# Dense attention with a subtracted maximum: reductions over 1024 keys, the maxima carried by DMA as one row, and the sums of the exponentials added up by a pair of half-width products

## The chip, the cores and the metric

The kernel runs on one core of a Trainium2 chip. The metric is the device time of one execution in microseconds (us), the median of several runs. Matrix products run on TensorE (PE in the profile; PEld is its weight loading), the other arithmetic on VectorE (DVE), ScalarE (ACT) and GpSimd (POOL). All transfers of the part discussed here are issued on one queue, that of SyncE (SP), in program order.

## The reference, cut to what matters

Two layers of a diffusion backbone, 2048 tokens behind a prefix of 256 context tokens, width 1024. The change lies in the dense attention of the first layer: 8 query heads of 64 channels share 2 key/value heads, and every query sees 2304 keys (256 context keys, then 2048 others). Context queries see the 256 context keys alone.

```python
def dense_attn(q, k, v):
    ...
    qg = q.reshape(Bq, Lq, Hk, Hq // Hk, dh)
    s = jnp.einsum('bqkgd,bskd->bkgqs', qg, k).astype(jnp.float32) * (dh ** -0.5)
    p = jax.nn.softmax(s, axis=-1).astype(v.dtype)
    o = jnp.einsum('bkgqs,bskd->bqkgd', p, v)
    return o.reshape(Bq, Lq, Hq * dh)
```

The softmax is computed with the row's maximum subtracted before the exponential and the row's sum divided out after the product with the values. The program keeps scores with the opposite sign, so that the maximum is a minimum (`ALU.min`), and `AF.Exp` runs with scale -1.

## The kernel before, in words

The program runs its phases one after another: `ab_proj` (input projection, convolution), `ab_attention`, `ab_out`, then the second layer. Only `load_kv` and `ab_attention` are touched.

**Units.** The work is cut into 36 units in the list `units` (L850 to L852), one for 256 queries of two query heads: 512 columns of queries. 32 units see 18 tiles of 128 keys; four (block 0, the context queries) see 2 tiles. They run one after another, 584 tiles in all.

**What one tile of keys costs.** `score` (L902) multiplies one tile of keys by the unit's 512 queries into one PSUM bank of the pool `ps_s` (two banks, used in turn). It is two products: one over 128 rows with the rounded queries and keys, and one over the tile `qm` and the low part of the keys, whose last rows add the (negated) maximum: the keys' tile has rows of ones there (L803), `qm` has the shift. `exp` on ACT (L912) reads the bank and writes `pr`. `multiply` (L915) takes two tiles of `pr` at a time: the values of either tile have 64 columns, so that the two products fill the two halves of the array's columns and land in partitions 0 to 63 and 64 to 127 of one bank (`ps_a`). `add` (L932) adds up the `pr` tiles, some on DVE (`accd`), the rest on POOL (`accp`).

**The maxima ahead of it.** `chunk` (L876) computes the rounded scores the other way round, 128 queries in the partitions and up to 512 keys in the columns, into one of three banks (`ps_m`), and DVE reduces each to one column (L886). A unit has 4 tiles of queries by 5 chunks (four of 512 keys, one of 256). `least` (L888) takes the least of five columns. `shift_row` (L892) transposes the [128, 4] result on PE into a bank of the pool `ps_r`, and one DVE instruction spreads it, times an identity, over the rows 64 to 67 of `qm`.

**The sums behind it.** `join` (L949) adds `accd` and `accp` on POOL. `sum_high` and `sum_low` split the sum into two rounded parts on ACT and DVE. `total` (L966) multiplies both by a column of ones into the bank of `ps_r` (one row of 512 sums), ACT copies the row, and a transfer (L980) spreads it over 128 partitions. `invert` (L982) takes the reciprocal, writes it to DRAM (L987) and reads it back broadcast over 128 partitions (L989). `divide`, `fold` and `store` (L991 to L1007) finish the unit on POOL and ACT. In the last unit `total` uses 128 columns of ones and inverts the full tile on DVE.

**What sets the order.** The instructions of TensorE, ScalarE, VectorE and GpSimd are issued in an order written out by hand: every tile of keys is one step, `at(step, order, f)` files each piece of work under a step and a rank within it (L1009 to L1036), and L1079 to L1085 emit them step by step, ranks in ascending order (maxima and their rows 0, 1, 4, 5; score and exponential 2; multiply 3; add 6; the unit's tail 7). The tail's distances from the unit's last step `e` stand in `CHAIN`; `RATE` is the number of steps from one chunk to the next, and a unit's last chunk is `AHEAD` = 7 steps before its first score. The order on SP is chosen by a scheduler. `extra` (L1058) fits other work into the same steps: conditioning products (`adaln`), writes of a bias table to DRAM (`patterns`, L268), the output projection's weights, and parts of the convolution's normalization.

PSUM has eight banks: three for chunks, two for scores, one for the product with the values, one for rows (`ps_r`), one for the other work (`ps_c`).

Of the kernel before, what the change touches and what calls it, by code (L numbers as in the profile page):

```python
# [83 lines left out]
class Build:  # L84
# [705 lines left out]
    def load_kv(self):  # L790

        nc = self.nc
        self.kv_es = ExitStack()
        kp = self.pool(self.kv_es, "kp", 1, side="right")
        self.kt = []
        for kv in range(2):
            rows = slice(kv * 64, kv * 64 + 64)
            hi = kp.tile([P, T], F32R, name=f"k{kv}h")
            lo = kp.tile([68, T], F32R, name=f"k{kv}l")
            for r in range(2):  # L800
                nc.sync.dma_start(hi[r * 64 : r * 64 + 64].bitcast(F32), self.k_d[0, rows])
            nc.sync.dma_start(lo[0:64].bitcast(F32), self.k_d[1, rows])
            nc.vector.tensor_copy(  # L803
                lo[64:68].rearrange("p (a n) -> p a n", n=P),
                self.ones[64:68].unsqueeze(1).broadcast_to((4, NT, P)),
            )
            self.kt.append((hi, lo))
        self.vt = kp.tile([P, NT, P], F32, name="vt")
        nc.sync.dma_start(self.vt[:], self.v_d[:].rearrange("i p n -> p i n"))

    def ab_attention(self):
# [7 lines left out]
        with ExitStack() as es:  # L819
# [9 lines left out]
            tp = self.pool(es, "apt", 6)  # L829
# [13 lines left out]
            onesr = rp.tile([P, P], F32R, name="onesr")  # L843
            nc.vector.tensor_copy(onesr[:], self.ones[:])
            AHEAD, LAG, SUM, RATE, ROW = 7, 3, 2, 0.85, 4
# [3 lines left out]
            CHAIN = (5, 7, 9, 11, 14, 19, 21, 22)  # L849
# [12 lines left out]
            def load_q(i):  # L862
                b, hp = units[i]
                qs = qp.tile([P, 2, 256], F32R, name="q", tag="q")
                for j in range(2):
                    nc.sync.dma_start(qs[:, j].bitcast(F32), self.qs_d[2 * hp + j][:, b * 256 : b * 256 + 256])
                st = sp.tile([P, 4, 6], F32, name="ast", tag="ast")
                state[i] = {"q": qs, "st": st}

            def load_high(i):  # L870
                b, hp = units[i]
                qm = state[i]["qm"] = mp.tile([68, 2, 256], F32R, name="qm", tag="qm")
                for j in range(2):
                    nc.sync.dma_start(qm[0:64, j].bitcast(F32), self.qs_d[2 * hp + j][0:64, b * 256 : b * 256 + 256])

            def chunk(i, qt, c):  # L876

                b, hp = units[i]
                s = state[i]
                a = c * 512  # L880
                n = min(512, tiles[i] * P - a)
                lhs = s["q"][:, qt // 2, (qt % 2) * P : (qt % 2) * P + P]
                ps = ps_m.tile([P, 512], F32, name="m", tag="m")
                nc.tensor.matmul(ps[:, :n], lhs, kt[hp // 2][0][:, a : a + n], start=True, stop=True)  # L884
                col = c if b else 5
                nc.vector.tensor_reduce(out=s["st"][:, qt, col : col + 1], in_=ps[:, :n], axis=AX.X, op=ALU.min)  # L886

            def least(i):  # L888
                st = state[i]["st"]
                nc.vector.tensor_reduce(out=st[:, :, 5:6], in_=st[:, :, 0:5], axis=AX.X, op=ALU.min)  # L890

            def shift_row(i):  # L892
                s = state[i]
                pt = ps_r.tile([P, 512], F32, name="row", tag="row")
                nc.tensor.transpose(pt[0:4, 0:P], s["st"][:, :, 5], self.ident[:])
                nc.vector.scalar_tensor_tensor(
                    out=s["qm"][64:68].rearrange("p j (i n) -> p (j i) n", n=P),
                    in0=pt[0:4, 0:P].unsqueeze(1).broadcast_to((4, 4, P)), scalar=-1.0,
                    in1=self.ident[0:4, 0:4].unsqueeze(2).broadcast_to((4, 4, P)), op0=ALU.mult, op1=ALU.mult,
                )  # L900
# [14 lines left out]
            def multiply(i, k):  # L915
                b, hp = units[i]
                s = state[i]
                if k == 1:
                    s["av"] = ps_a.tile([P, 512], F32, name="av", tag="av")
                kv = hp // 2  # L920
                for x in range(2):
                    nc.tensor.matmul(  # L922
                        s["av"][x * 64 : x * 64 + 64], vt[:, k - 1 + x, kv * 64 : kv * 64 + 64], s["pr"][k - 1 + x][:],
                        start=k == 1, stop=k == tiles[i] - 1,
                    )
# [5 lines left out]

            def add(i, k):  # L932

                s = state[i]
                n = tiles[i]
                if n == 2:
                    mine, eng, name = [0, 1], nc.vector, "accd"
                else:
                    dve = [3 * x + 2 for x in range(5)] + [16, 17] if i < len(units) - 1 else list(range(TAIL, n))
                    mine, eng, name = (dve, nc.vector, "accd") if k in dve else ([x for x in range(n) if x not in dve], nc.gpsimd, "accp")  # L940
# [8 lines left out]
            def join(i):  # L949
                s = state[i]  # L950
                if "accp" in s:
                    nc.gpsimd.tensor_tensor(out=s["accd"][:], in0=s["accd"][:], in1=s["accp"][:], op=ALU.add)

            def sum_high(i):
                s = state[i]
                s["sh"] = rp.tile([P, 512], F32R, name="sh", tag="sh")
                nc.scalar.activation(s["sh"][:], s["accd"][:], AF.Copy)

            def sum_low(i):
                s = state[i]  # L960
                s["sl"] = rp.tile([P, 512], F32R, name="sl", tag="sl")
                nc.vector.tensor_tensor(
                    out=s["sl"][:], in0=s["accd"][:], in1=s["sh"][:].bitcast(F32), op=ALU.subtract
                )

            def total(i):  # L966

                s = state[i]
                pt = ps_r.tile([P, 512], F32, name="row", tag="row")
                m = 1 if i < len(units) - 1 else P  # L970
                for x in ("sh", "sl"):
                    nc.tensor.matmul(pt[0:m], onesr[:, 0:m], s[x][:], start=x == "sh", stop=x == "sl")
                if m == P:
# [3 lines left out]
                row = rp.tile([1, 512], F32, name="srow", tag="srow")  # L977
                nc.scalar.activation(row[:], pt[0:1], AF.Copy)
                s["rc"] = sp.tile([P, 4], F32, name="rc", tag="rc")
                nc.sync.dma_start(s["rc"][:], row[0:1].rearrange("o (p f) -> o p f", f=4))  # L980

            def invert(i):  # L982
# [3 lines left out]
                nc.vector.reciprocal(s["rc"][:], s["rc"][:])  # L986
                nc.sync.dma_start(self.inv_d[i % 2].rearrange("o (p f) -> (o p) f", f=4), s["rc"][:])  # L987
# [23 lines left out]
            for i in reversed(range(len(units))):  # L1011
                chunks = [(qt, c) for qt in range(4) for c in range(5 if units[i][0] else 1)]
                time = min(time - RATE, first[i] - AHEAD)
                last = int(time // 1)
                for x in reversed(chunks):
                    at(int(time // 1), 4, bind(chunk, i, *x))
                    begin = int(time // 1)
                    time -= RATE
                time += RATE
                at(begin - 3, 0, bind(load_q, i))  # L1020
                at(last - 2, 0, bind(load_high, i))
                if units[i][0]:
                    at(last + 1, 5, bind(least, i))
                at(last + ROW, 1, bind(shift_row, i))
            for i, n in enumerate(tiles):
                for k in range(n):
                    s = first[i] + k
                    at(s, 2, bind(score, i, k))
                    if k % 2 == 1:
                        at(s + LAG + 0, 3, bind(multiply, i, k))  # L1030
# [865 lines left out]
```

## Time and profile before

| | us |
|---|---|
| three runs | 2920.73, 2907.32, 2914.79; median 2914.79 |
| the profiled execution | 2907.36, of it the span of the profile 2905.6 |
| first score product of the attention | at 703.4 of the span |
| last score product of the attention | at 1532.7 |
| mean granted TensorE clock over the span | 0.977 |

In the profile's groups a line gives the source line, engine, operation, the tiles written and read, their shapes, a count, then the busy time in us and the mean duration of one instruction in ns, then the engine's idle time ahead of that group and what ended it. A product counts as busy until its modelled end, although the next one can start earlier: the distance between two starts is what a product costs on PE when PE is the limit. In a timeline the columns are the start in us, the duration in us, engine, line and operation; "x4" merges four of a kind. The table by stretches gives the busy time of each engine in each stretch, then the granted clock, the busy share of the DMA engines and GB/s.

### The profile page before, as it was taken

Reading aid. Unit: us, or ns where it says so; the run is one execution under the profiler, and the core shown is the slowest. Engines: PE = TensorE matmul, PEld = TensorE weight load, DVE = VectorE, ACT = ScalarE, POOL = GpSimd, SP = SyncE. Lnnn points to the kernel's source line nnn. Section 1 sums busy time; section 2 is a strip of 40 time slices with the busy share of each in tenths; the row PEclk is TensorE's granted clock in tenths of the full one; section 3 lists DMA queues with packets and bytes.
Section 4 is the critical chain, followed back from the end, with each engine's and each line's share of the span. In section 5 each row is a group of like instructions: output and inputs, shape, how many; then the busy total and the mean of one; then the engine's idle time right before and its main releaser. Section 6 shows DMA issues by size and latency. Waiting matters only on the chain.

```text
span 2905.6 us, 40946 instructions
## 1 busy us (share of the span) xinstructions
PE 2752.1 (95%) x14481; PEld 2118.0 (73%) x14481; DVE 1825.2 (63%) x2867; ACT 1116.8 (38%) x2081; POOL 1416.4 (49%) x1151
## 2 busy tenths in 40 slices
PE   7998799999999999999999999999999997889898
PEld 5988799996444444444447788988898876788787
DVE  4798868898777878878977454101212246777563
ACT  3223120312445555555553223123222236677321
POOL 2568610711666787887885652222222214445342
PEclk9999899998999999999999999999999998999999
DMA  9546332474533433321216543333434269998862
GB/s 297 192 131 207 129 123 97 135 239 151 149 107 103 144 98 106 120 68 44 73 33 210 192 159 143 138 112 112 143 132 136 82 197 230 235 230 196 270 210 80
DMA packets 346808, 432.27 MB, mean 149 GB/s; under 512 B 55900, under 2 KB 260236, under 8 KB 341611
## 3 DMA queue, kind: packets, MB, share of 16 engines
q1 hardware_dynamic: 310891, 403.03, 46.2%
q10 hardware_dynamic: 35712, 26.62, 2.9%
q8 instruction: 114, 1.87, 0.3%
q14 instruction: 91, 0.75, 0.1%
HBM read 281.87 MB, written 152.84 MB: 150 GB/s over the span
## 4 chain that ended last, share of the span: by engine, by line
PE 62%; DMA 10%; DVE 3%; POOL 2%; issue 2%; ACT 1%; SPq 0%; POOLq 0%; ACTq 0%; DVEq 0%
PE av L922 9%; PE s L907 8%; PE mm L431 6%; PE mm L433 6%; PE mm L432 6%; PE m L884 6%; PE mo L1107 4%; PE mo L1108 4%; PE mo L1109 4%; DMA nv<-v_d 3%; DMA nk<-k 3%; PE mm L442 1%; PE mm L441 1%; PE mm L440 1%; DMA pat<-pat_d 1%
## 5 line engine op out<-in xcount | busy, mean ns | idle before, releaser
L886 DVE TENSOR_REDUCE ast<-m 128x1 f32<-128x512 f32 (+1 forms) x656 | 397.9, 626 | 145.9 <-PE m L884 143.8
L912 ACT ACTIVATE pr<-s 128x512 f32<-128x512 f32 x584 | 343.2, 595 | 311.7 <-PE s L907 269.6
L947 POOL TENSOR_TENSOR accp<-accp,pr 128x512 f32<-128x512 f32 x283 | 400.1, 1414 | 86.0 <-ACT pr L912 71.3
L447 POOL TENSOR_TENSOR wlo<-wraw,whi 128x1024 fp32r<-128x1024 f32 x64 | 202.4, 3169 | 380.3 <-ACT whi L446 380.2
L533 DVE SCALAR_TENSOR_TENSOR acc<-u,cw,acc 128x1151 f32<-128x1151 f32 (+1 forms) x240 | 353.0, 1526 | 0.0
L922 PE MATMUL av<-pr,vt 128*64 128x512 f32 x1168 | 315.7, 619 | 0.0
L433 PE MATMUL mm<-hi_ab,wlo 128*128 128x384 f32 x768 | 258.7, 338 | 16.8 <-POOL wlo L447 15.5
L432 PE MATMUL mm<-lo_ab,whi 128*128 128x384 f32 x768 | 259.8, 339 | 0.0
L431 PE MATMUL mm<-hi_ab,whi 128*128 128x384 f32 x768 | 256.2, 340 | 3.3 <-ACT hi_ab L380 1.9
L431 PE MATMUL mm<-hi_cd,whi 128*128 128x512 f32 x640 | 250.8, 392 | 1.1 <-ACT hi_cd L380 1.1
L432 PE MATMUL mm<-lo_cd,whi 128*128 128x512 f32 x640 | 250.1, 391 | 0.4 <-DVE lo_cd L381 0.4
L433 PE MATMUL mm<-hi_cd,wlo 128*128 128x512 f32 x640 | 246.7, 390 | 0.0
L947 DVE TENSOR_TENSOR accd<-accd,pr 128x512 f32<-128x512 f32 x165 | 169.2, 1026 | 1.3 <-DVE accd L947 0.5
L1664 DVE TENSOR_TENSOR nlo<-npt,nhi 128x512 fp32r<-128x512 f32 x192 | 123.6, 645 | 69.3 <-ACT nhi L1662 68.5
L884 PEld LDWEIGHTS m<-k1h,q 128*128 128x128 f32 x328 | 61.8, 188 | 133.8 <-DVE ast L886 79.8
L433 PEld LDWEIGHTS mm<-hi_ab,wlo 128*128 128x128 f32 x768 | 145.5, 190 | 17.8 <-POOL wlo L447 15.8
L884 PEld LDWEIGHTS m<-k0h,q 128*128 128x128 f32 x328 | 63.5, 196 | 125.2 <-DVE ast L886 82.1
L1626 POOL TENSOR_SCALAR npr<-npr,nst 128x640 f32<-128x640 f32 (+1 forms) x128 | 108.0, 857 | 89.5 <-DVE nst L1625 64.1
L372 DVE TENSOR_SCALAR ht<-ptr,scale,shift 128x384 f32<-128x384 f32 (+2 forms) x96 | 61.2, 671 | 141.1 <-PE ptr L369 140.5
L431 PEld LDWEIGHTS mm<-hi_ab,whi 128*128 128x128 f32 x768 | 144.9, 190 | 5.3 <-ACT hi_ab L380 2.9
L432 PEld LDWEIGHTS mm<-lo_ab,whi 128*128 128x128 f32 x768 | 145.4, 189 | 0.9 <-issue 0.8
L431 PEld LDWEIGHTS mm<-hi_cd,whi 128*128 128x128 f32 x640 | 120.4, 188 | 26.1 <-ACT hi_cd L380 1.6
(321 smaller groups left out, 6931.4 us busy)
## 6 DMA issues: line engine op xcount, KB each, us to landing
wraw<-in_cd_w_in_dram SPq DMA_DIRECT2D x46, 512.0 KB, 3.8
pat_d<-big SPq DMA_DIRECT2D x72, 256.0 KB, 4.0
nk<-k SPq DMA_DIRECT2D x32, 576.0 KB, 12.7
pat<-pat_d SPq DMA_DIRECT2D x24, 768.0 KB, 6.0
nv<-v_d SPq DMA_DIRECT2D x128, 128.0 KB, 7.3
adaraw<-in_ab_w_ada_dram SPq DMA_DIRECT2D x24, 512.0 KB, 8.2
adaraw<-in_cd_w_ada_dram SPq DMA_DIRECT2D x24, 512.0 KB, 3.7
w_d<-whi SPq DMA_DIRECT2D x22, 512.0 KB, 2.8
```

Of the source, the lines that this page charges most:

```text
L431: nc.tensor.matmul(ps, a, hh[:, k, cols], start=k == 0, stop=False)
L432: nc.tensor.matmul(ps, a, hl[:, k, cols], start=False, stop=False)
L433: nc.tensor.matmul(ps, b, hh[:, k, cols], start=False, stop=k == KT - 1)
L447: (eng or nc.vector).tensor_tensor(out=lo, in0=src, in1=hi.bitcast(F32), op=ALU.subtract)
L533: ins = nc.vector.scalar_tensor_tensor(out=acc[:, :n], in0=u[:, tap : tap + n], scalar=cw[:, ch, tap : tap + 1], in1=acc[:, :n], op0=ALU.m ...
L884: nc.tensor.matmul(ps[:, :n], lhs, kt[hp // 2][0][:, a : a + n], start=True, stop=True)
L886: nc.vector.tensor_reduce(out=s["st"][:, qt, col : col + 1], in_=ps[:, :n], axis=AX.X, op=ALU.min)
L907: nc.tensor.matmul(ps[:], kt[hp // 2][key][:, k * P : k * P + P], s[x][:].rearrange("p j n -> p (j n)"), start=key == 0, stop=key == 1,)
L912: nc.scalar.activation(pr[:], ps[:], AF.Exp, scale=-1.0)
L922: nc.tensor.matmul(s["av"][x * 64 : x * 64 + 64], vt[:, k - 1 + x, kv * 64 : kv * 64 + 64], s["pr"][k - 1 + x][:], start=k == 1, stop=k == ...
L947: eng.tensor_tensor(out=s[name][:], in0=first_in[:], in1=s["pr"][k][:], op=ALU.add)
L1664: return lambda: nc.vector.tensor_tensor(out=lo[:, :o], in0=pt[:, :o], in1=hi[:, :o].bitcast(F32), op=ALU.subtract)
```

## The change

Maxima: a chunk covers two banks, 1024 keys of one tile of queries, in two products and one reduction. The 256 context keys of all four tiles of queries make one more chunk (four products, one reduction over each quarter). A unit has 9 chunks instead of 20, one every second step. The pool of chunk banks holds two tiles of two banks.

The row: one DVE instruction takes the least of three columns, a second negates it into the [128, 4] tile `sr`, and four transfers on SP carry a column of 128 values each into row 64 of `qm`. The transpose on PE, the spreading instruction on DVE, the pool `ps_r` and three of the four rows of ones are gone.

The sums: the joining on POOL and the split on ACT and DVE are gone. `total` multiplies `accd` and `accp`, unrounded, each by 64 columns of ones, side by side in the two halves of the array, into one bank taken from the pool of the scores, `ps_s`. `spread` copies 65 rows of it (rows 0 and 64 are the two partial sums), two transfers spread them over partitions, `invert` adds the two and goes on as before. In a unit of two tiles the two `pr` tiles themselves take the place of the partial sums. The tail's distances change: the total is 7 steps behind the unit's last tile instead of 11, the inversion 11 instead of 14, the division 17 instead of 19. There are nine `pr` tiles instead of six, and DVE adds other tiles than before.

```diff
-            lo = kp.tile([68, T], F32R, name=f"k{kv}l")
+            lo = kp.tile([65, T], F32R, name=f"k{kv}l")
...
-            tp = self.pool(es, "apt", 6)
+            tp = self.pool(es, "apt", 9)
...
-            ps_m = self.pool(es, "psm", 3, PSUM)
+            ps_m = self.pool(es, "psm", 2, PSUM)
...
-            ps_r = self.pool(es, "psr", 1, PSUM)
...
-            AHEAD, LAG, SUM, RATE, ROW = 7, 3, 2, 0.85, 4
+            AHEAD, LAG, SUM, RATE = 7, 3, 2, 2
...
-            CHAIN = (5, 7, 9, 11, 14, 19, 21, 22)
+            CHAIN = (3, 7, 8, 11, 17, 19, 20)
...
-            def chunk(i, qt, c):
+            def chunk(i, c):
...
+                ps = ps_m.tile([P, 1024], F32, name="m", tag="m")
+                key = kt[hp // 2][0]
+                if b and c < 8:
+                    parts = [(c // 2, c % 2 * 1024 + x * 512, 512) for x in range(2)]
+                else:
+                    parts = [(qt, 2048 if b else 0, 256) for qt in range(4)]
+                for x, (qt, a, n) in enumerate(parts):
+                    lhs = s["q"][:, qt // 2, (qt % 2) * P : (qt % 2) * P + P]
+                    nc.tensor.matmul(ps[:, x * n : x * n + n], lhs, key[:, a : a + n], start=True, stop=True)
+                if len(parts) == 2:
+                    nc.vector.tensor_reduce(
+                        out=s["st"][:, c // 2, c % 2 : c % 2 + 1], in_=ps[:], axis=AX.X, op=ALU.min
+                    )
...
             def shift_row(i):
...
+                row = sp.tile([P, 4], F32R, name="sr", tag="sr")
+                nc.vector.tensor_scalar(out=row[:], in0=st[:, :, 3], scalar1=-1.0, scalar2=None, op0=ALU.mult)
+                for qt in range(4):
+                    to = s["qm"][64:65, qt // 2, (qt % 2) * P : (qt % 2) * P + P].bitcast(F32)
+                    nc.sync.dma_start(to.rearrange("o (n f) -> o n f", f=1), row[:, qt : qt + 1].bitcast(F32))
...
+            def by_dve(i):
+                return [2, 4, 8, 10, 14, 16, 17] if i < len(units) - 1 else list(range(TAIL, NT))
...
             def total(i):
 
                 s = state[i]
-                pt = ps_r.tile([P, 512], F32, name="row", tag="row")
...
+                pt = s["tot"] = ps_s.tile([P, 512], F32, name="s", tag="s")
...
+                for x, name in enumerate(("accd", "accp")):
+                    nc.tensor.matmul(pt[x * 64 : x * 64 + 64], self.ones[:, 0:64], s[name][:], start=True, stop=True)
+
+            def spread(i):
...
+                row = rp.tile([65, 512], F32, name="srow", tag="srow")
+                nc.scalar.activation(row[:], s["tot"][0:65], AF.Copy)
+                s["rc"] = sp.tile([P, 2, 4], F32, name="rc", tag="rc")
+                for x in range(2):
+                    nc.sync.dma_start(s["rc"][:, x], row[64 * x : 64 * x + 1].rearrange("o (p f) -> o p f", f=4))
...
+                at(last, 5, bind(shift_row, i))
...
-                at(e + LAG, 4, bind(unload, i))
-                ds = {len(units) - 2: CHAIN[:5] + (22, 24, 25), len(units) - 1: (2, 4, 4, 8, 8, 9, 10, 11)}.get(i, CHAIN)
-                for d, f in zip(ds, (join, sum_high, sum_low, total, invert, divide, fold, store)):
+                ds = CHAIN if i < len(units) - 1 else (3, 4, 4, 4, 8, 9, 10)
+                for d, f in zip(ds, (unload, total, spread, invert, divide, fold, store)):
                     at(e + d, 7, bind(f, i))
```

More of the change, by code (lines that the diff above doesn't have):

```diff
@@ L871, in load_high @@
                 b, hp = units[i]
-                qm = state[i]["qm"] = mp.tile([68, 2, 256], F32R, name="qm", tag="qm")
+                qm = state[i]["qm"] = mp.tile([65, 2, 256], F32R, name="qm", tag="qm")
                 for j in range(2):
                     nc.sync.dma_start(qm[0:64, j].bitcast(F32), self.qs_d[2 * hp + j][0:64, b * 256 : b * 256 + 256])
-            def chunk(i, qt, c):
+            def chunk(i, c):
                 b, hp = units[i]
                 s = state[i]
[L880 to L886, printed above, removed]
@@ L895, in shift_row @@
[L895 to L900, printed above, removed]
+                st = s["st"]
+                if units[i][0]:
+                    nc.vector.tensor_reduce(out=st[:, :, 3:4], in_=st[:, :, 0:3], axis=AX.X, op=ALU.min)
@@ L930, in unload @@
                 nc.scalar.activation(s["o"][:], s["av"][:], AF.Copy)
+            def by_dve(i):
+                return [2, 4, 8, 10, 14, 16, 17] if i < len(units) - 1 else list(range(TAIL, NT))
             def add(i, k):
                 s = state[i]
[L935 to L940, printed above, removed]
+                if tiles[i] == 2:
+                    s["accd" if k == 0 else "accp"] = s["pr"][k]
+                    return
+                dve = by_dve(i)
+                mine, eng, name = (dve, nc.vector, "accd") if k in dve else ([x for x in range(NT) if x not in dve], nc.gpsimd, "accp")
                 x = mine.index(k)
@@ L947, in add @@
                 eng.tensor_tensor(out=s[name][:], in0=first_in[:], in1=s["pr"][k][:], op=ALU.add)
[L949 to L964, printed above, removed]
             def total(i):
                 s = state[i]
[L969 to L973, printed above, removed]
+                pt = s["tot"] = ps_s.tile([P, 512], F32, name="s", tag="s")
+                if i == len(units) - 1:
+                    for x in ("accp", "accd"):
+                        nc.tensor.matmul(pt[:], self.ones[:], s[x][:], start=x == "accp", stop=x == "accd")
                     s["r"] = rp.tile([P, 512], F32, name="r", tag="r")
```

45 lines of the change are left out of this document (20 added, 25 removed).

## The prediction

> **What bounds the kernel now.** I first read the page's table of engines and the table by stretches, cut at the attention.
>
> ```profile
> span 2905.6 us, 40946 instructions
> PE 2752.1 (95%) x14481; PEld 2118.0 (73%) x14481; DVE 1825.2 (63%) x2867; ACT 1116.8 (38%) x2081; POOL 1416.4 (49%) x1151
> ...
> 690.00:1100.00 410.00, 407.35 (x1782) 194.62 (x1783) 318.47 (x515) 207.20 (x378) 273.10 (x218) 0.98 0.43 126
> 1100.00:1540.00 440.00, 424.45 (x1666) 201.82 (x1666) 374.25 (x546) 239.68 (x424) 349.23 (x260) 1.00 0.25 75
> sum 850.00, PE 831.80 PEld 396.44 DVE 692.73 ACT 446.88 POOL 622.34; mean PE 415.90 PEld 198.22 DVE 346.36 ACT 223.44 POOL 311.17
> ...
> 1530.00:1600.00 70.00, 70.00 (x311) 55.83 (x310) 48.70 (x59) 23.38 (x39) 41.58 (x36) 1.00 0.65 221
> ```
>
> The attention lasts some 850 us, and the first number behind a stretch's length is PE's busy time: 831.80 of 850, so PE is idle 18.2 us in all. DVE is busy 692.73, POOL 622.34, ACT 446.88. PE is the limit here. In the stretch behind it PE is busy 70.00 of 70, so a later end of the attention is passed on. What the change takes off DVE, POOL and ACT can therefore give back little more than those 18.2 us; what it puts on PE or makes PE wait for is paid in full.
>
> A busy time of PE can hide short gaps, so I read starts in the timeline, in a stretch without visible idle time:
>
> ```profile
> 1181.71 0.40 PE L907 MATMUL s<-qm,k1l 68*128 68x512 f32 x1
> ...
> 1182.04 1.08 PE L922 MATMUL av<-pr,vt 128*64 128x512 f32 x4
> ...
> 1182.20 0.60 ACT L912 ACTIVATE pr<-s 128x512 f32<-128x512 f32 x1 [0.40 <-PE s L907]
> ...
> 1183.05 0.50 PE L884 MATMUL m<-k1h,q 128*128 128x512 f32 x1
> ...
> 1183.38 0.39 PE L907 MATMUL s<-q,k1h 128*128 128x512 f32 x1
> ...
> 1183.58 0.69 DVE L886 TENSOR_REDUCE ast<-m 128x1 f32<-128x512 f32 x1 [0.61 <-PE m L884]
> 1183.62 0.40 PE L907 MATMUL s<-qm,k1l 68*128 68x512 f32 x1
> ...
> 1183.85 0.39 PE L884 MATMUL m<-k1h,q 128*128 128x512 f32 x1
> ...
> 1184.09 0.39 PE L907 MATMUL s<-q,k1h 128*128 128x512 f32 x1
> ...
> 1184.64 1.08 PE L922 MATMUL av<-pr,vt 128*64 128x512 f32 x4
> ```
>
> A rounded product of 512 columns takes 0.23 (1183.62 to 1183.85), or 0.33 right behind or right before the values' product; a pair of half-width products of unrounded data (x4) takes 1.01 (1182.04 to 1183.05). From one pair to the next, two steps, it is 2.60. Products stand start to start: nothing is waited for.
>
> **The sums, on PE.** Gone are two rounded products in each of 35 units, 0.24 each by the distance of the starts below, 35 x 0.48 = 16.8, and the transposes, 36 times something between nothing and their duration of 0.278; they lie between other products, so I take 0.1, 3.6.
>
> ```profile
> 970.94 0.40 PE L972 MATMUL row<-sh,onesr 128*1 128x512 f32 x1
> 971.18 0.39 PE L972 MATMUL row<-sl,onesr 128*1 128x512 f32 x1
> ...
> L895 PE MATMUL row<-ident,ast 128*4 128x128 f32 x36 | 10.0, 278 | 0.0
> L972 PE MATMUL row<-sl,onesr 128*1 128x512 f32 x35 | 13.7, 392 | 7.8 <-DVE sl L962 7.8
> ```
>
> Added are 35 column-tiled pairs. They have the form of the values' pair, 128 rows by 64 columns, 512 unrounded columns streamed, so 35 x 1.01 = 35.4. The last unit's two products of 128 columns do not run side by side; they cost between 0.46 as now and 2.0, and I take 1.5 more. Sum: 35.4 + 1.5 - 16.8 - 3.6 = **+16.5**.
>
> **The sums, in the scores' banks.** The total now takes one of the two banks through which scores pass in turn, and this is the dearest part. In steps from the unit's end e: score e+7 uses bank B, the total behind it A, score e+8 B, score e+9 A again. So score e+9 waits until `spread` has read A, and `spread` is filed at e+8 with rank 7, behind the exponential of e+8 with rank 2, on an engine that works in order. From the start of the second product of score e+8: the exponential starts after 0.49 (1181.71 to 1182.20), takes 0.60, and the copy takes the 0.585 of the row copy of today, which has as many columns:
>
> ```profile
> L978 ACT ACTIVATE srow<-row 1x512 f32<-1x512 f32 x35 | 20.5, 585 | 50.4 <-PE row L972 46.0 <-DMA rc<-srow 3.2 <-DMA pat_d<-toep 1.2
> ```
>
> That frees the bank after 1.68. In this time PE has the rest of that product, 0.23, and the chunk of the step, 2 x 0.23; e is odd and chunks fall on odd steps, the values' products on even ones, so nothing else stands between. PE waits 1.68 - 0.69 = 0.99. Times 35 it is **+35**; where no chunk is left, in the last unit, 0.46 more. Everything behind on PE stands: chunk, values, the next unit's scores. The bounds are nothing (if the scores come late anyway) and 1.5 x 35 = 52 (no chunk in the gap). I take 35, since no idle time on PE stands in the way of it. The Trainium skill, TensorEngine Tiling (Array Packing), section PSUM Bottleneck, says that tiling speeds up TensorE but not the emptying of PSUM, so that the copy out can become the limit. By it alone the pair would be cheap and the copy the price, the same 35; the rows of ACT decide.
>
> **The maxima.** Chunks stream the same columns. DVE's reductions follow from two rows:
>
> ```profile
> L886 DVE TENSOR_REDUCE ast<-m 128x1 f32<-128x512 f32 x512 | 342.3, 685 | 111.0 <-PE m L884 109.0
> L886 DVE TENSOR_REDUCE ast<-m 128x1 f32<-128x256 f32 x141 | 58.8, 417 | 31.3 <-PE m L884 31.1
> L890 DVE TENSOR_REDUCE ast<-ast 128x4 f32<-128x20 f32 x32 | 5.3, 165 | 0.0
> L884 PE MATMUL m<-k0h,q 128*128 128x512 f32 x254 | 109.3, 457 | 4.3 <-DVE ast L886 4.2
> L884 PE MATMUL m<-k1h,q 128*128 128x512 f32 x256 | 108.4, 439 | 3.0 <-DVE ast L886 2.7
> ```
>
> 256 keys more cost 0.268, so 1024 take 0.685 + 2 x 0.268 = 1.22. A unit has 9 x 1.22 = 11.0 instead of 16 x 0.685 + 4 x 0.417 = 12.6. DVE has room, so this is worth only PE's waits for it: 4.2 + 2.7 above. A chunk bank is now asked for again two chunks or four steps later, 5.2 us, against 0.53 to the start of the reduction and 1.22 for it; these waits should go. With the 7.8 for the split that is 14.7, and part of it lies ahead of the stage or comes back as waits for late sums: **-12** (0 to -18). A product of 256 keys costs 0.12 to 0.23 today, depending on what follows:
>
> ```profile
> 867.02 0.28 PE L884 MATMUL m<-k0h,q 128*128 128x256 f32 x1
> ...
> 867.14 0.40 PE L907 MATMUL s<-q,k0h 128*128 128x512 f32 x1
> ```
>
> Four in a row could be at the lower end every time: 0 to -0.4 in 32 units, and I take **-5**.
>
> **The row by DMA.** Gone are 36 spreading instructions on DVE, added a negation of some 0.17 and four transfers. Their nearest rows are the sums' transfers today:
>
> ```profile
> rc<-srow SPq DMA_DIRECT2D x35, 2.0 KB, 2.0
> r<-inv SPq DMA_DIRECT2D x35, 256.0 KB, 4.0
> ...
> 1140.12 3.34 SPq L276 DMA_DIRECT2D pat_d<-toep  x4
> 1148.62 0.52 SPq L980 DMA_DIRECT2D rc<-srow  x1
> 1153.69 0.33 SPq L987 DMA_DIRECT2D inv<-rc  x1
> 1155.09 0.33 SPq L989 DMA_DIRECT2D r<-inv  x1
> ```
>
> From the last chunk's product to the landed row: 0.23 + 0.53 to the reduction, 1.22, 0.165 for the least of three, 0.17, four issues of 0.52 and 2.0 to the landing, 6.4 us. From step f-7 to f there are 3.5 x 2.60 = 9.1, so 2.7 are left and the usual row is hidden. What uses them up is SP, which works in order: a burst of four table writes takes 3.34, and the broadcast of the inverse waits 1.40 for its write (1153.69 to 1155.09) with the rows perhaps behind it. A burst comes every eight steps while the table is written. A third of the units late by 0.5 gives **+6**. On the queue, the row's transfers are followed by the loads of queries for later units, which have steps to spare; the second sum's transfer adds 0.52 on SP. `invert` keeps its three steps behind the copy; if it waits for its transfers, the additions and reductions behind it on DVE wait too, and PE only after the 3 us of slack in the chunk banks.
>
> **Free edits.** The joining on POOL, the rounding on ACT and the split on DVE go; none is the limit. The division comes six steps behind the inversion instead of five. Nine `pr` tiles leave ACT less to wait for. 65 rows instead of 68 stream as many columns. The start loses 24 reductions of at most 0.685 for ten of at most 1.22, and gains the transfers: 0.
>
> **Sum.** 16.5 + 35 - 12 - 5 + 6 = +40.5, say +40. The profiled execution took 2907.36 with its span of 2905.6, so 2947; the median of the runs, 2914.79, lies 7.4 above that execution, so I give **2955**. Its own range: a stall of 25 to 52, rows 0 to 25, the two gains at either end, 2925 to 3000.
>
> **Rivals.** *The stall is hidden* (0.22): scores e+9 come late for another reason, or the copy is early. Then +5, 2920, no change. For it, ACT is idle often; against it, ACT's order is fixed and PE has no idle time to lend.
>
> *Faster* (0.10): DVE, not PE, sets the pace in the second half, where it is busy 374.25 of 440.
>
> ```profile
> L896 DVE SCALAR_TENSOR_TENSOR qm<-row,ident 4x512 fp32r<-4x512 f32 x36 | 24.6, 682 | 1.5 <-PE row L895 0.4
> L962 DVE TENSOR_TENSOR sl<-accd,sh 128x512 fp32r<-128x512 f32 x36 | 36.6, 1016 | 1.3 <-ACT sh L957 1.3
> ```
>
> A unit's reductions, spreading and split take 12.6 + 0.165 + 0.68 + 1.02 = 14.5 on DVE before, and 11.0 + 0.165 and two small ones of 0.17 after, 11.5. If the some 17 units of that half became shorter by these 3.0, it would be -51 there, PE's stall hidden, and half of +40 in the first half: -31, 2884. It decides where PE's products stand apart because DVE frees their banks late. Against it: DVE ends only 14.7 us of PE's idle time, and the starts above, 0.23 apart, lie in that half.
>
> *The row is late* (0.13): each us beyond the 2.7 of slack costs PE 1 us in every unit. A landing of 4.0, as the broadcast has, and a blocked queue make it 2 late: +70 more, 3025. The Trainium skill, DMA: Bandwidth & Descriptors, section Specifications, says that pieces under 512 B are handled by read-modify-write, and these are 4 B into one partition; by that rule the rows would land later than the 2.0 measured for 16 B pieces. No transfer of data in the trace has such pieces, so it stays open.
>
> The forecast itself has 0.55. About 0.5%, 14.6 us, is what a measurement can tell from no change. Of the forecast's 0.55, 0.05 falls within that; of the hidden stall's 0.22, 0.17, with 0.03 slower and 0.02 faster; of the faster rival's 0.10, 0.01. So faster 0.11, same 0.23, slower 0.66. The range of 2908 to 3000 leaves out the faster rival and half of the late rows.
>
> **What would show it.** Right: one gap of about 1 us on PE in each unit, at a score product released by the copy of the sums' row; sums as groups of four, 1.01 to the next start; reductions of 1024 near 1.22; few PE waits for DVE. Wrong: no such gap at the score two behind a total; PE's idle time below 18 us; or gaps at the first low product of a unit, released by the row's transfer, which is the third rival.

## The result, and the profile after

The kernel after takes 2934.15 us (median of six executions, 2930.12 to 2939.03) against 2911.78 before (six, 2906.8 to 2920.73): ratio 1.0074 [1.0052, 1.0097], 22.4 us slower. The forecast was 2955, 40 slower, in a range of 2908 to 3000. The side was right, the size was not, and the parts behind it were partly wrong in opposite directions. The profiled execution of after took 2939.03, the slowest of its six; that of before, 2907.36, lies near the fastest. The two traces therefore differ by 31.7 us, 9 more than the medians.

First the page of the kernel after, and the tables by stretches, cut at the parts of the stage: from the projection's last product to the end of the second unit (the start), and from there to the last of the products with the values (the middle). Before the changed kernel's rows stand those of the kernel before:

```profile
span 2937.2 us, 40895 instructions
PE 2762.9 (94%) x14517; PEld 2117.4 (72%) x14517; DVE 1736.1 (59%) x2497; ACT 1104.6 (38%) x2045; POOL 1364.5 (46%) x1119
...
684.70:729.70 45.00, 40.44 (x145) 20.81 (x144) 37.68 (x63) 14.71 (x25) 13.04 (x10) 0.81 0.65 199
729.70:1534.90 805.20, 787.79 (x3286) 372.07 (x3284) 652.88 (x996) 433.34 (x779) 606.51 (x464) 1.00 0.32 94
...
688.80:750.60 61.80, 37.98 (x142) 19.52 (x142) 30.09 (x32) 14.44 (x24) 14.55 (x11) 0.78 0.51 146
750.60:1565.60 815.00, 801.01 (x3322) 374.64 (x3320) 569.80 (x660) 421.55 (x747) 550.49 (x433) 1.00 0.34 94
```

Both parts together take 876.8 us instead of 850.2. In the start the loss is idle time of PE, 23.8 us instead of 4.6. In the middle the idle time falls, from 17.4 to 14.0, and PE's busy time rises by 13.2: there the loss lies in more work and in gaps too short to count. The prediction had nothing at the start, and a gap of about 1 us in every unit. Who ends the idle time stands in the waits of PE, from the stage's start to its last unit, before and then after:

```profile
PE row L972 <- DVE sl L962: 7.8, 6, 2.6
PE m L884 <- DVE ast L886: 7.0, 7, 3.6
PE s L907 <- ACT pr L912: 5.4, 5, 2.0
```

```profile
PE s L911 <- DMA qm<-qs: 17.0, 1, 17.0
PE s L911 <- ACT pr L916: 7.3, 33, 0.3
PE s L911 <- DMA qm<-sr: 4.7, 4, 2.8
PE m L885 <- DVE ast L887: 3.2, 7, 0.9
...
PE m L885 <- DVE ast L891: 1.6, 1, 1.6
PE s L911 <- DMA pat_d<-big: 1.2, 1, 1.2
```

(Columns: total us, times, longest.) The waits for DVE, 14.8 us (4.3 of them in the start), have shrunk to 4.8. In their place stand one wait of 17.0 us, 33 short ones for ACT, and some for the row. The group of the new reductions in the kernel after:

```profile
L887 DVE TENSOR_REDUCE ast<-m 128x1 f32<-128x1024 f32 x256 | 312.3, 1223 | 249.9 <-PE m L885 248.9
```

A reduction of 1024 takes 1.223 us (forecast 1.22).

**The total and the two scores behind it**, in the timeline of the kernel after:

```profile
1221.09 0.59 PE L967 MATMUL s<-accd,ones 128*64 128x512 f32 x1
...
1222.04 0.50 PE L911 MATMUL s<-q,k1h 128*128 128x512 f32 x1
...
1222.62 0.63 PE L885 MATMUL m<-k1h,q 128*128 128x512 f32 x2
1222.81 0.60 ACT L916 ACTIVATE pr<-s 128x512 f32<-128x512 f32 x1 [1.87 <-PE s L911]
...
1223.31 0.58 ACT L975 ACTIVATE srow<-s 65x512 f32<-65x512 f32 x1
...
1223.46 0.50 PE L911 MATMUL s<-q,k1h 128*128 128x512 f32 x1 [0.21 <-ACT pr L916]
```

The pair takes 0.95 from start to start (1221.09 to 1222.04; forecast 1.01). Score e+8 begins at 1222.04, two products of the chunk follow at 1222.62, and score e+9 could start 0.47 later, at 1223.09. It starts at 1223.46, so it waits 0.37, not 0.99 (the row's 0.21 counts only from the modelled end of the product before it; so the 7.3 in the waits are less than what these gaps cost). It is released by the exponential of score e+8, which ends at 1222.81 + 0.60 = 1223.41; the copy of the total ends only at 1223.89. So score e+9 doesn't take the total's bank, which is still being read. Of the two banks it takes the other, which comes free first, that of score e+8.

**The start.** SP's issues and PE's first low products in the kernel after:

```profile
702.27 0.17 DVE L901 TENSOR_SCALAR sr<-ast 128x4 fp32r<-128x4 f32 x1
...
707.77 0.94 SPq L227 DMA_DIRECT2D adaraw<-in_ab_w_ada_dram  x2
...
714.45 3.50 SPq L904 DMA_DIRECT2D qm<-sr  x4
...
724.14 0.29 PEld L911 LDWEIGHTS s<-qm,k0l 65*128 65x128 f32 x1 [17.67 <-DMA qm<-sr]
724.17 0.76 PE L911 MATMUL s<-qm,k0l 65*128 65x512 f32 x1 [16.98 <-DMA qm<-qs]
724.73 0.63 PE L911 MATMUL s<-q,k0h 128*128 128x512 f32 x1
725.16 0.63 PE L911 MATMUL s<-qm,k0l 65*128 65x512 f32 x1
```

The second unit's row is ready on DVE at 702.44. SP, which is loading weights of 512 KB a piece, comes to its four transfers at 714.45; they are issued by 717.95 and PE starts at 724.17. The product's releaser is named by the other half of the same tile; its weight load names the row, and e5 below shows that it is the row. Once PE runs again, its rounded products stand 0.43 apart instead of 0.23.

In parts, measured in the traces (us): from the last product of the projection to the end of the second unit 45.0 before, 61.8 after (**+16.8**); from there to the last product of values 805.2 and 815.0 (**+9.8**); from there to the first product of the stage behind the output projection 211.5 and 219.2 (**+7.7**). What lies behind, 1159.1 and 1152.5, and ahead, 684.7 and 688.8, isn't touched; in all traces of this study the first of these varies from 1148 to 1160. A unit of 18 steps that nothing disturbs takes, from its first score product to the next unit's, 24.01 before and 24.76 after.

### The profile page after: what moved, and what is told of

Its sections match the earlier page's. It is cut to its first block, busy times and chain, and to the rows that moved or that the text cites. A ratio compares the mean times of both kernels' runs of the same rounds, so it can differ in the third digit from the quotient of the medians.

```text
span 2937.2 us, 40895 instructions
## 1 busy us (share of the span) xinstructions
PE 2762.9 (94%) x14517; PEld 2117.4 (72%) x14517; DVE 1736.1 (59%) x2497; ACT 1104.6 (38%) x2045; POOL 1364.5 (46%) x1119
## 4 chain that ended last, share of the span: by engine, by line
PE 63%; DMA 11%; DVE 2%; ACT 1%; issue 1%; SPq 1%; POOL 1%; POOLq 0%; DVEq 0%; ACTq 0%
PE s L911 10%; PE av L927 9%; PE mm L431 6%; PE mm L433 6%; PE mm L432 6%; PE mo L1104 4%; PE mo L1102 4%; PE mo L1103 4%; DMA nv<-v_d 4%; PE m L885 4%; DMA nk<-k 2%; PE mm L442 1%; PE mm L441 1%; PE mm L440 1%; PE s L967 1%
## 5 line engine op out<-in xcount | busy, mean ns | idle before, releaser
L887 DVE TENSOR_REDUCE ast<-m 128x1 f32<-128x1024 f32 x256 | 312.3, 1223 | 249.9 <-PE m L885 248.9
L954 DVE TENSOR_TENSOR accd<-accd,pr 128x512 f32<-128x512 f32 x165 | 158.7, 962 | 3.1 <-ACT pr L916 2.5
L911 PEld LDWEIGHTS s<-q,k1h 128*128 128x128 f32 x292 | 54.8, 188 | 133.1 <-ACT pr L916 109.6
L911 PEld LDWEIGHTS s<-q,k0h 128*128 128x128 f32 x292 | 55.3, 189 | 119.1 <-ACT pr L916 91.9
```

The source lines that it names most:

```text
L887: nc.vector.tensor_reduce(out=s["st"][:, c // 2, c % 2 : c % 2 + 1], in_=ps[:], axis=AX.X, op=ALU.min)
L911: nc.tensor.matmul(ps[:], kt[hp // 2][key][:, k * P : k * P + P], s[x][:].rearrange("p j n -> p (j n)"), start=key == 0, stop=key == 1,)
```

## The experiments

Theory A: the time after is made of the row's transfers behind a blocked SP at the start, the copy of the total standing behind an exponential, and late rows later on, less what the maxima gain. The rivals stand with each run. Times are medians, ratios are to the kernel before in the same session, whose medians lay between 2910.4 and 2912.3.

**e1, another queue for the first rows.**

```
- nc.sync.dma_start(to..., row...)
+ (nc.scalar if i < 2 else nc.sync).dma_start(to..., row...)
```

> The changed kernel, but the row transfers of the first two units are issued on ScalarE's queue instead of SyncE's. Theory A: the 17.4 us in which TensorE waits at the first low product of the second unit come from the place of those four transfers in SyncE's order, behind 512 KB loads; then this wait shrinks to 1 to 3 us and the time falls by 15 to 19, to about 2917. Rival B: the wait is the load of that unit's queries itself, late because the DMA engines are full, and moving the row changes it by less than 3 us; time within 4 us of the changed kernel.

2931.97, 1.0072 [1.0059, 1.0085]: a miss for theory A as far as SP's order goes, and the time that rival B gave; e5 tells whether it is B's cause. The start stays at 60.5. In the timeline of e1 ACT's queue is now the one that is stuck:

```profile
695.00 0.17 DVE L901 TENSOR_SCALAR sr<-ast 128x4 fp32r<-128x4 f32 x1
...
702.95 5.09 ACTq L904 DMA_DIRECT2D qm<-sr  x4
708.07 1.28 ACT L916 ACT_TABLE_LOAD   x1 [25.86 <-DMA adaraw<-in_cd_w_ada_dram]
...
710.02 0.79 PE L911 MATMUL s<-q,k0h 128*128 128x512 f32 x1 [12.94 <-ACT pr L916]
...
714.64 0.77 PE L911 MATMUL s<-qm,k0l 65*128 65x512 f32 x1 [3.83 <-DMA qm<-sr]
```

The second unit's row is ready at 695.17, but ACT issues its four transfers only from 702.95 to 708.04, and the exponentials stand behind them. By the trace's releasers, each of the four goes out when an earlier transfer has landed: the first behind a load of queries, the others behind weight loads that were issued 6 to 8 us before. So it isn't SP's order alone: the row's transfers wait for loads that land late. The engines of the transfers are full at that time; the table by stretches of the kernel after, with their share and the GB/s as the last two numbers, has it so while the row is on its way:

```profile
717.00:721.00 4.00, 0.00 (x0) 0.00 (x0) 0.00 (x0) 0.00 (x0) 0.00 (x0) 0.50 1.03 257
```

**e5, the first rows without a transfer.** For the first two units four products with the identity put the row into a chunk bank, and one DVE instruction negates it into `qm`:

```
+ for qt in range(4):
+     nc.tensor.matmul(ps[64:65, qt * P : qt * P + P], s["st"][:, qt, 3:4], self.ident[:], start=True, stop=True)
+ nc.vector.tensor_scalar(out=s["qm"][64:65]..., in0=ps[64:65, 0:512], scalar1=-1.0, ...)
```

> The changed kernel, but the row of the first two units is made by four products with the identity into a chunk bank and one instruction on VectorE, without a transfer; all other units by transfers as before. Theory A, mended after the run with another queue: the wait of 13 to 17 us at the second unit comes from the DMA engines, which are full with 512 KB loads from 701 to 719 us, so that any transfer that the stage needs there is late, on whichever queue; without one the second unit ends about 45 us behind the projection, as before the change, instead of 61.8, and the time falls by 14 to 17, to about 2918. Rival B: the load of the second unit's queries is just as late, and PE still waits over 10 us there; within 4 us of the changed kernel.

2920.8, 1.0036 [1.0019, 1.0053]: 13.4 less than after. The start falls from 61.8 to 42.0, below that of before; the rest of the stage keeps its 815.9. Theory A held, rival B didn't, and the start was the row's.

**e2, the copy one step earlier.**

```
- CHAIN = (3, 7, 8, 11, 17, 19, 20)
+ CHAIN = (3, 7, 7, 11, 17, 19, 20)
```

> The changed kernel, but the copy of the sums' row is filed at e+7 instead of e+8, so that ScalarE does it ahead of the exponential of step e+8. Theory A: the wait of 0.37 to 0.45 at the score product of step e+9 in each unit is a wait for the exponential of e+8, whose bank it reuses since the total's bank is given back later; with the copy earlier, that score takes the total's bank, and the wait goes: 33 times 0.4, 13 us, to about 2921; a clean unit falls from 24.76 to about 24.35. Rival B: the exponential of e+8 now comes 0.6 later, so that the wait moves to score e+10; time unchanged within 4 us.

2922.23, 1.0041 [1.0028, 1.0054]: 11.9 less than after. The undisturbed unit goes from 24.76 to 24.29, the stretch from 815.0 to 801.2. In the timeline of e2 the copy (1207.71) now stands ahead of the exponential of score e+8 (1208.34), and score e+9 no longer waits. It starts at 1208.61, ahead of that exponential's end at 1208.94, so it now has the total's bank:

```profile
1207.71 0.59 ACT L975 ACTIVATE srow<-s 65x512 f32<-65x512 f32 x1 [1.25 <-PE s L967]
...
1208.34 0.60 ACT L916 ACTIVATE pr<-s 128x512 f32<-128x512 f32 x1
...
1208.61 0.40 PE L911 MATMUL s<-q,k1h 128*128 128x512 f32 x1
```

**e6, two more steps for the maxima.**

```
- AHEAD, LAG, SUM, RATE = 7, 3, 2, 2
+ AHEAD, LAG, SUM, RATE = 9, 3, 2, 2
```

> The changed kernel with the last chunk nine steps ahead of a unit's first score instead of seven, so that a row has 2.6 us more to land. Theory A: outside the first units 5 or 6 of 35 rows are late by 0.3 to 2.9 us, 7 us in all, and a wait of 2.9 us is followed by some 3 us of products at half the pace; both go, 7 to 10 us less, about 2926; the wait at the second unit stays. Rival B: the rows are late because of what stands ahead of them on SyncE, whatever the lead; unchanged within 4 us.

2924.34, 1.0049 [1.0032, 1.0067]: 9.8 less than after. The stretch goes from 815.0 to 805.3, and of PE's waits between 735 and 1520 only the bank's are left, 33 of them as before the edit.

What made a row late is seen in the longest case of the kernel after, in the timeline and in the table by stretches:

```profile
1253.60 0.34 SPq L987 DMA_DIRECT2D inv<-rc  x1
1255.39 0.52 SPq L904 DMA_DIRECT2D qm<-sr  x1
1256.32 0.33 SPq L989 DMA_DIRECT2D r<-inv  x1
1256.70 1.99 SPq L276 DMA_DIRECT2D pat_d<-big  x4
1258.73 2.74 SPq L904 DMA_DIRECT2D qm<-sr  x3
...
1264.50 0.80 PE L911 MATMUL s<-qm,k1l 65*128 65x512 f32 x1 [2.76 <-DMA qm<-sr]
```

```profile
1265.00:1267.00 2.00, 2.00 (x5) 0.30 (x4) 0.00 (x0) 1.43 (x3) 0.50 (x1) 0.50 0.63 156
```

The broadcast of the inverse waits for its write, a burst of four table writes follows, and three of the row's four transfers stand behind both, as the prediction had it. What it lacked is the price: after the 2.76 the granted clock (the number behind the five engines) is 0.50 up to 1271, and that unit takes 30.87 instead of 24.76, 6.1 more with a wait of 2.76.

**e8, all rows by products.** As e5, for all 36 units.

> The changed kernel with every row made by four products with the identity into a chunk bank and one instruction on VectorE of about 0.7 us; no transfer of a row is left. Theory A: the start gains 15 and the late rows 7 to 10, and the products cost 36 times 0.4 to 0.6, 14 to 22 on TensorE: between 2925 and 2934, so the transfers are no dearer than the products over the whole stage, and it is the first 20 us that make them dear. Rival B: the transfers also cost in ways that no wait at the low product shows (SyncE's order, other loads late): 2915 or less.

2958.97, 1.0172 [1.015, 1.0194], above what either theory gave. No row is late, but the undisturbed unit is 25.94, 1.18 longer than after. The timeline of e8 shows what four small products cost PE:

```profile
1303.32 1.03 PE L912 MATMUL m<-ident,ast 128*1 128x128 f32 x8
1304.28 0.50 PE L922 MATMUL s<-q,k1h 128*128 128x512 f32 x1
```

They take 0.96, more than the 0.4 to 0.6 expected. The middle takes 848.0 instead of 815.0: there the transfers are the cheaper way, and only at the start the dearer one.

**e3, the sums alone**, and **e11**, the same with the copy a step earlier: the kernel before with the pair, its copy, the new steps of the chain, nine `pr` tiles and the new choice of tiles for DVE.

```
+ pt = s["tot"] = ps_s.tile([P, 512], F32, name="s", tag="s")
+ for x, name in enumerate(("accd", "accp")):
+     nc.tensor.matmul(pt[x * 64 : x * 64 + 64], self.ones[:, 0:64], s[name][:], start=True, stop=True)
e3:  CHAIN = (3, 7, 8, 11, 17, 19, 20)
e11: CHAIN = (3, 7, 7, 11, 17, 19, 20)
```

> The kernel before with the sums of the changed one (column-tiled pair into a bank of the scores, nine exponential tiles, the new tail distances and tiles added on VectorE), but the maxima as before: 512 keys a chunk, three banks, transposed on TensorE. Theory A: a clean unit costs about 0.45 more TensorE time for the pair and up to 0.4 of waiting for the scores' bank, 32 x 0.85 = 27, less 10 to 15 us of waits for the split and for late additions that go: 12 to 17 us slower than before, about 2926. Rival B: the sums cost nothing net, and all of the 22 us come with the maxima: within 5 us of before.

> The new sums alone, in the kernel before, with spread filed at e+7 instead of e+8. Theory A: of the 25.52 of e3's undisturbed unit, 0.6 is the score's wait for the copy, the rest the pair: 24.9, time 2910 to 2920 (0.9995 to 1.003). Rival B: the wait isn't the copy's but the exponentials' behind it, and comes back at another score: the unit stays at 25.3 or more, time 2928 to 2938 (1.006 to 1.009).

e3 took 2932.95, 1.0073 [1.0058, 1.0087], more than expected; e11 2915.85, 1.0022 [1.0006, 1.0038], as theory A has it. The undisturbed unit falls from 25.52 to 24.87. PE's waits for ACT in the stage, of e3 and of e11:

```profile
PE s L905 <- ACT pr L910: 13.7, 33, 0.5
```

```profile
PE s L905 <- ACT pr L910: 0.4, 1, 0.4
```

So the place of the copy, one number in a list, is worth 17.1 us here. It also shows that the wait comes with the new sums and not with the new maxima.

**e4, the maxima alone**, and two attempts to mend it: the kernel before with the new maxima and the row by DMA; the sums are joined, rounded and split as before, but their total goes into a bank of the scores, since the chunk banks now take all four banks.

```
e4:  CHAIN = (4, 5, 6, 7, 11, 17, 19, 20)
e10: e4 with the first rows of e5, AHEAD 9, CHAIN = (4, 6, 7, 9, 13, 18, 20, 21)
e12: e10 with CHAIN = (4, 6, 7, 9, 12, 19, 21, 22), the last unit but one at 22, 24, 25
```

> The changed maxima (1024 keys, row by DMA) with the sums of before (joined on GpSimd, split into two rounded parts, two products with one column of ones), whose total stands in a bank of the scores since no other is left, at step e+7, with six exponential tiles. Theory A: the wait at the second unit stays (17 us) and a few late rows (7 us), reductions wait less (-7): 12 to 18 us slower than before, about 2927, nearly all of it in the first 50 us of the attention. Rival B: the maxima are free and the sums carry the loss: within 5 us of before, and the first wait is an accident of one execution.

> The maxima over 1024 keys alone, the sums joined, rounded and split as before, but without what got in the way in e4: the rows of the first two units by products, AHEAD 9, and the chain of the sums later (total at e+9, not e+7). Theory A: what e4 lost lay in the start, the late rows and the early total, and the maxima themselves gain PE's waits for DVE and the 256-key products: the undisturbed unit 24.1, the stretch from the second unit to the last values 785 to 800, time 2890 to 2908 (0.992 to 0.999). Rival B: a total in a bank of the scores costs as much with the split as with the pair, wherever it stands: the undisturbed unit stays at 24.5 or more, time 2915 to 2935 (1.001 to 1.008).

> e10 with the inversion at e+12 instead of e+13, the division and what follows one step later (e+19, e+21, e+22), and the last unit but one's at e+22, e+24, e+25 as in the kernel before. Theory A: in e10 the division waited on POOL up to 5.9 us for the landed inverse, ACT's fold for it up to 3.7 us, and the exponentials behind it; PE's waits of 1 to 2.1 us for these halved its pace for some us after each. With seven steps from inversion to division instead of five these go: nearly all units take 23.8 (the undisturbed one of e10), the stretch from the second unit to the last values 785 to 800, time 2875 to 2900 (0.988 to 0.9965). Rival B: in the first half the inverse lands late because the engines of the transfers are full, however long one waits: units of 28 to 30 stay there, time 2915 or more.

e4 took 2951.44, 1.0130 [1.0113, 1.0147]; e10 2933.04, 1.0078 [1.0054, 1.0102]; e12 2916.54, 1.0014 [1.0000, 1.0027]. All three are slower than theory A expected, and e10 and e12 took the times of rival B, so none shows the maxima cleanly. What they do show: the undisturbed unit of e10 and e12 is 23.77, 0.24 below that of before, and the stretch of e12 is 797.6 against 805.2. What keeps them back seems to be the chain of the sums in its new place. ACT's waits of e12 between 735 and 1520, and PE's:

```profile
ACT sh L975 <- POOL accd L970: 32.0, 29, 3.3
```

```profile
PE s L924 <- ACT pr L929: 15.9, 17, 1.8
```

The rounding waits on ACT for POOL's join in 29 units, exponentials stand behind it, and PE waits for exponentials 17 times. No run changes the join alone, so this is read from the waits and not tested. Behind the last unit e12 loses 16.1 more than before (227.6 against 211.5). The maxima alone with the old steps of the chain weren't tried, so what they are worth by themselves is known for an undisturbed unit only.

**e7, together**: the copy of e2, the rows of e5, AHEAD 9 as in e6, and TAIL 10, which gives DVE fewer additions in the last unit.

> The changed kernel with the copy of the sums one step earlier, the first two rows by products, nine steps of lead, and the last unit's additions split 10 to 8 between GpSimd and VectorE instead of 6 to 12. Theory A: the gains add: 12 for the copy, 15 for the start, 7 for the late rows, 3 for the end of the stage: 37 less than the changed kernel, about 2897, and 10 to 17 faster than the kernel before. Rival B: they overlap, since PE regains in later waits what it saves: about 2912, no different from before.

2894.29, 0.9945 [0.9924, 0.9966]: faster than both kernels, 39.9 less than after. The parts measured singly give 11.9 + 13.4 + 9.8 = 35.1; the other 4.8 can't be put down to TAIL: the first output product still comes 3.8 behind the last of the values, where it is 3.6 in e5 and e6, which leave TAIL as it was. Of PE's waits in the stage of e7 this is the largest item; 2.7 more are for DVE:

```profile
PE s L922 <- ACT pr L927: 4.1, 4, 2.5
```

## Why the prediction was right, and where wrong

**The sums' pair: right.** 0.95 for 1.01. With the new maxima the undisturbed unit is 24.29 with the pair (e2, e7) and 23.77 with the two rounded products (e10): 0.52 a unit, where 35.4 - 16.8 over 35 units forecasts 0.53. With the old maxima it is dearer: e11's unit is 0.86 above that of before, and there a chunk's rounded product stands between the values' pair and the sums'.

**The products of 256 keys and the transposes: right.** Forecast -5 and -3.6; the unit of e10, 0.24 shorter than that of before, gives -7.7 over 32 units.

**The scores' banks: the step that failed.** "Score e+7 uses bank B, the total behind it A, score e+8 B, score e+9 A again." The wait is there, at the right score, in 33 units, and it goes when the copy goes ahead (e2). But the bank is not the next in turn; it is the one whose reader comes first on ACT, and that is freed by the exponential, one copy earlier. With the copy ahead (e2) it is the total's. The term of +35 is 11.9 by the times of e2 and 13.8 by its trace. Had the prediction taken the exponential's end, 0.49 + 0.60, less 0.69 of work, it would have had 0.40 a unit, 14, and a sum of +19.5.

**PE's waits for DVE: right by the waits, but something beside them was left out.** Forecast -12; by the waits above, 14.8 less 4.8, 10.0 are gone. In e7, where no row is late and the bank is waited for 4 times instead of 33, the middle is 12.7 shorter than before although each of 32 units is 0.28 longer without disturbance, 9.0. So 21.7 have gone from the middle, and the waits for DVE in that part of before are only 10.5 of it. Another part is seen in one unit of before, of 27.77: behind a wait of 1.53 for an exponential, which ends at 1270.82, its granted clock is 0.50 (shown at the end). What the rest is stays open.

**The row by DMA: cause right, size low.** Forecast +6, 9.8 by e6. Of this the waits for late rows make 5.9 (4.7 and the 1.2 for `pat_d`); the slower clock behind the longest, 6.1 - 2.76 = 3.3, makes most of the rest.

**The start: put at 0, a second step that failed.** The step "gains the transfers: 0" left out that the engines of the transfers are full there. It cost 16.8 in the trace, 13.4 by the times of e5. The prediction costed the row by SP's queue in the middle of the stage and not by SP's queue at its first use, with weights of 512 KB on it.

**The last unit: 1.5 forecast, 4.2 found.** The 1.5 was for dearer products; what the trace shows is another cost. In the kernel after the last total stands in PE's order ahead of the output products and waits for DVE's additions:

```profile
1561.05 8.54 DVE L954 TENSOR_TENSOR accd<-accd,pr 128x512 f32<-128x512 f32 x7
...
1569.64 1.12 PE L962 MATMUL s<-accd,ones 128*128 128x512 f32 x2 [1.61 <-DVE accd L954]
1570.20 0.80 PE L1102 MATMUL mo<-wout,yh 128*128 128x512 f32 x1
```

The first output product comes 4.6 after the last of the values, against 0.4 before. Of the +7.7 up to the next stage 3.5 stay unexplained; with the same tail this part took 215.0 in e6 and 220.0 in e1, so it is not clear of scatter.

**The sum.** The parts of the middle, in the traces, are 9.0 + 13.8 - 21.7 + 9.7 = 10.8, against +9.8 found; as 21.7 is a remainder, this only shows that the copy and the rows add up. So the bank was too dear by 23, and what leaves the middle too small by some 10; the start, too cheap by 13 to 17, partly made up for it. Without the start's cost, which the prediction didn't have, the kernel after is only 9 slower (e5, 2920.8 against 2911.9): that the forecast came as near as it did is in part luck.

**The rivals.** The late row came true at the start and at a few bursts, not in every unit. Its reason from pieces under 512 B doesn't set the rows apart, since the sums' 16 B pieces lie under 512 B too, and no run varies the pieces alone. The rival of a hidden stall had the nearest figure, 2920, by another way than what happened. The rival on the faster side didn't come true; e7, another kernel, is faster by 17.6, but nothing shows that DVE set the pace before: its undisturbed unit, 24.29, is longer than that of before.

## What to carry to other kernels

Where a tile of another kind is put into a pair of banks in use, ask which bank comes free first, and put the instruction that frees the odd one ahead of the next regular one on its in-order engine: here one step is worth 12 to 17 us. A transfer that is hidden in the steady part has to be costed again at its first use, where the queue and the engines carry the loads of the stage's start. And a PE wait of 2 to 3 us can cost about twice its length, when the granted clock falls behind it.

## What was not expected of the hardware

The granted clock can fall after short waits. In the kernel after it was 0.50 behind a wait of 2.76 us, for 6 us. In e10 it fell behind one of 1.84; the timeline of e10, and its table by stretches:

```profile
796.07 0.74 PE L924 MATMUL s<-q,k0h 128*128 128x512 f32 x1 [1.84 <-ACT pr L929]
```

```profile
794.00:796.00 2.00, 0.23 (x1) 0.00 (x0) 1.74 (x2) 1.41 (x4) 1.40 (x3) 1.00 0.54 156
796.00:798.00 2.00, 1.93 (x4) 0.74 (x6) 0.30 (x1) 1.87 (x5) 1.92 (x2) 0.54 0.81 221
```

The Trainium skill, TensorE: Matmul & The Clock Gate, section HAM oscillation — how this bites in real kernels, says that PE should have no idle gap of more than some 3.4 us, or it falls back to half its clock. The half agrees; the length doesn't: here 1.84 and 2.76 were enough. Nor does the length alone decide. In the kernel before the clock fell behind a wait of 1.53 (to 1270.82) and not behind one of 2.57 (to 1426.62):

```profile
1272.00:1274.00 2.00, 2.00 (x6) 0.35 (x5) 0.65 (x1) 0.78 (x2) 1.84 (x3) 0.50 0.05 16
1427.00:1429.00 2.00, 2.00 (x10) 0.74 (x9) 1.70 (x4) 1.67 (x3) 1.92 (x2) 1.00 0.44 149
```

What else decides is not shown. A wait of 1.21 (the one for `pat_d` in the waits of after) cost its unit 1.47 in all (26.23 against 24.76), hardly more than itself.

With the engines full, four small transfers kept ACT's queue from 702.95 to 708.04 (e1), after 7.8 us in which it held the finished row; in the kernel after SP issues four in 3.50. And products with a single output row are not small for PE: four of 128 unrounded columns take 0.96 (e8), as long as the sums' pair of 512.
